# Holding Down's rows behind the product in the first feed-forward, and three of its tiles in the wide form

## The chip, the cores and the metric

The kernel runs on one core of a Trainium2 chip. The metric is the device time of one execution in microseconds (us), lower is better, as the median of several runs. PE is the tensor engine, DVE the vector engine, ACT the scalar engine, POOL the engine that issues some of the DMAs, SP the one that issues the others. PEld is the loading of weights into PE, which has its own rows in the trace.

## The reference

One decoder layer on 512 tokens of width 1024, in float32: a SwiGLU feed-forward, a mixer (dilated attention with 12 heads beside a gated linear recurrence), and a second SwiGLU feed-forward. Around each stand two RMS norms. The part that the change touches:

```python
def swiglu(x, w_gate, w_up, w_down):
    return (jax.nn.silu(x @ w_gate) * (x @ w_up)) @ w_down

f = swiglu(rms_norm(h, ffn1_norm_pre[l]), ffn1_w_gate[l], ffn1_w_up[l], ffn1_w_down[l])
h = h + 0.5 * rms_norm(f, ffn1_norm_post[l])
```

`w_gate` and `w_up` are 1024 x 2816, `w_down` is 2816 x 1024. 2816 is 22 tiles of 128 columns.

## The kernel before, in words

**Numbers in two parts.** Each float32 operand is split into a high part of a reduced format and a low part, the remainder (`split`, lines 302 to 304: one copy on ACT, one subtraction on DVE). A product is then three matmuls: high by high, high by low, low by high.

**Seven products for eight.** From tile 6 on in the first feed-forward, from tile 3 on in the second, the gate and up products of a tile of 128 columns are made together as a 2 x 2 block product with seven half-sized products p1 to p7 (a Strassen-Winograd scheme). Each of the seven runs over four slices of 128 of the contraction and has 256 columns of tokens. The weights are combined on DVE and split on ACT and DVE into seven forms (`w_forms`, lines 681 to 702), a tile ahead of their use. Partial sums of the seven are chained through PSUM banks: one bank is copied into another, and the next product adds onto the copy.

**Two forms of a tile's product.** The narrow form (`seven_on`, with `seventh`, lines 722 to 733) takes, for each of the seven products and each slice, three matmuls of 256 columns, at lines 730 to 732: 7 x 4 x 3 = 84 in a tile. It uses four PSUM banks of the tag `acc`, which has five. The wide form (`seven_wide`, from line 764) takes two matmuls for a slice, at lines 782 and 783: the high weights against the high and low tokens side by side (512 columns, into the two halves of a bank), and the low weights against the high tokens (256 columns, into the second half): 7 x 4 x 2 = 56 in a tile. It needs all five banks; its two halves are added up when a bank is read, by `fold` (ACT line 794, DVE line 796), `sum_of` (DVE lines 804 and 806) and `move` (ACT line 788, 512 columns). In the kernel before the wide form is in the mixer's query and key products and in tiles 9, 13 and 17 of the second feed-forward.

**Down in four steps.** The tiles are grouped in parts: 0 to 3, 4 to 7, 8 to 11, 12 to 15, and 16 to 21. The product of Down with the first four parts is also made with seven products, in four steps spread over the tiles behind the part (`STEPS_AT`). A step has two, two, one and two of the seven products; each is two groups of six matmuls of 512 columns (lines 1065 to 1067) into a bank of the tag `aux`, which has three. So the steps have 24, 24, 12 and 24 matmuls. A group's bank is first filled with the running sum by ACT ("seeding", line 1053), and copied out by ACT behind the group (line 1070). Behind the last part the sums are put together on DVE (`merge`, lines 1081 to 1087). In the first feed-forward the tiles and steps go: tile 9 and step 0, tile 10 and step 1, tile 11 and step 2, tile 12 and step 3, tile 13 and step 0, and so on.

**What sets the order.** The program is written with a scheduling layer: it orders the instructions of each engine by dependencies, by the order in the text and by priorities (`tc.high_priority`), and it inserts the waits on semaphores. `tc.issue_after(x)` keeps what stands under it behind the instruction `x`. `state["product"]` is the last matmul of the tile's product. In the second feed-forward (`n == 2`) Down's matmuls are held behind it; in the first they are free, and the scheduler may put them between those of the product. Weights come from DRAM over SP's queue in the order in which they are used, 512 KB at a time, through four buffers `raw`.

The tiles' outputs go through `into`, which forms the left operands of Down: on DVE at lines 925 to 935, and `split`.

Of the kernel before, what the change touches and what calls it, by code (L numbers as in the profile page):

```python
# [20 lines left out]
NF = 22  # L21
FF_PARTS = ((0, 4), (4, 8), (8, 12), (12, 16), (16, 22))
NSTD = {1: 6, 2: 3}
WIDE = {1: (), 2: (9, 13, 17)}

SEVEN = range(4)
STEPS_AT = {1: ((6, 7, 7, 8), range(9, 13), range(13, 17), range(17, 21)),
# [157 lines left out]
def hybrid_layer(ctx: ExitStack, tc: tile.TileContext, xT: bass.AP, xN: bass.AP, wst: bass.AP,  # L185
# [47 lines left out]
    state = {"g": 0, "i": 0, "off": 0, "raw": None, "ahead": AHEAD, "split": None}  # L233
# [78 lines left out]
    def tmp(name):  # L312
        return tpool.tile([P, T], F32, name=name, tag="t")
# [550 lines left out]
    def ffn(n, x, r, forms_x, apool, pss):  # L864
# [96 lines left out]
        def prod(f, w):  # L961
            g, u = tmp("g"), tmp("u")
            if f in WIDE[n]:
                seven_wide(t, w, *([x[:, h] for h in HALVES] for x in (g, u)), then=forms_left)
# [69 lines left out]
        def sum_at(p):  # L1034
            if p in outs:
                o, half, sign = outs[p]
                return quarter(o, half), sign
            return acts["ea"][:, extra.index(p)], 1.0

        def follows(a, p):  # L1040

            return a > 0

        def groups(i):
            return [(p, k) for p in SEVEN_STEPS[i] for k in range(2)]

        def seed(a, p, k):
            if "ea" not in acts:
                acts["ea"] = apool.tile([P, 4, 2, T], F32, name="ea", tag="e", bufs=1)
            ps = seeded[p, k] = aux_ps()  # L1050
            if follows(a, p):
                src, sign = sum_at(p)
                ACT.activation(ps, src[:, k], AF.Copy, scale=sign)

        def down7(a, i, w):
            x = sevens[a]
            gs = groups(i)
            for m, (p, k) in enumerate(gs):
                ps = seeded.pop((p, k))
                first = not follows(a, p)  # L1060
                for j in range(2):
                    xh, xl = (x[p][:, s_, j * HB + k * P:j * HB + k * P + P] for s_ in range(2))
                    wh, wl = (w[p][:, s_, j * T:(j + 1) * T] for s_ in range(2))
                    with tc.issue_after(state["product"]) if n == 2 else nullcontext():
                        PE.matmul(ps, xh, wh, start=first and j == 0, stop=False, skip_group_check=True)  # L1065
                        PE.matmul(ps, xh, wl, start=False, stop=False, skip_group_check=True)  # L1066
                        PE.matmul(ps, xl, wh, start=False, stop=j == 1, skip_group_check=True)  # L1067
                dst, sign = sum_at(p)
                with tc.high_priority(offset=EVAC):
                    ACT.activation(dst[:, k], ps, AF.Copy, scale=sign)  # L1070
                    if m + 3 < len(gs):
                        seed(a, *gs[m + 3])
            if a == SEVEN[-1]:
                merge(i)

        def merge(i):

            p1, p7, p6, p5 = (acts["ea"][:, k] for k in range(4))
            if i == 1:
                DVE.tensor_add(quarter(0, 0), quarter(0, 0), p1)  # L1080
                DVE.tensor_add(p6, p6, p1)
                DVE.tensor_add(p7, p7, p6)
                DVE.tensor_sub(quarter(0, 1), quarter(0, 1), p7)
                DVE.tensor_add(quarter(2, 0), quarter(2, 0), p6)
            if i == 2:
                DVE.tensor_add(quarter(2, 0), quarter(2, 0), p5)
                DVE.scalar_tensor_tensor(quarter(2, 1), p7, -1.0, p5, op0=ALU.mult, op1=ALU.subtract)
# [4 lines left out]
        for ev in ffn_order(n):  # L1092
            if ev[0] == "std":
                j = ev[1]
                while len(pss) < 2 * j + 2:
                    pss.append(acc_ps())
                    gemm(pss[-1], fetch(keys[len(pss) - 1]), x)
                with tc.high_priority(offset=EVAC if j == NSTD[n] - 1 else 0):
                    std_out(pss[2 * j], pss[2 * j + 1], j)

                for step in steps[j:] if j == min(NSTD[n], 4) - 1 else steps[j:j + 1]:
                    step()
            elif ev[0] == "prep":
                with ExitStack() as edges:
                    while behind:
                        edges.enter_context(tc.issue_after(behind.pop()))
                    forms[ev[1]] = w_forms(("gu", n, ev[1]))
            elif ev[0] == "prepd":
                forms[ev[1:]] = d_forms(*ev[1:])
                if n == 2:  # L1110
                    behind[:] = [state["split"], state["low"]]
            elif ev[0] == "seeds":
                for g in groups(ev[2])[:3]:
                    seed(ev[1], *g)
            elif ev[0] == "down7":
                down7(*ev[1:], forms.pop(ev[1:]))
            else:
                prod(ev[1], forms.pop(ev[1]))
# [773 lines left out]
```

## Time and profile before

| | us |
|---|---|
| median of 3 runs | 1206.48 (1205.55 to 1207.29) |
| the profiled execution | 1206.06 |
| its span, first to last instruction | 1204.3 |
| PE busy in the span | 1196.5 |
| DVE busy | 1039.5 |
| ACT busy | 838.7 |
| mean granted clock of PE | 0.998 |

A row of the timeline gives the start, the duration and the instruction. Matmuls are pipelined: the duration of a row reaches beyond the start of the next, so what a matmul costs in a dense stretch is the distance from its start to the next one's start. In the table by windows, a row has the window, its length, and for each engine the busy time with the number of instructions. Times in the texts count from the start of the span. The products of tiles 6 to 21 of the first feed-forward lie between 71.9 and 309.6 us, those of the second between 897.2 and 1165.2 us.

### The profile page before, as it was taken

The numbers are of one execution on the slowest core, as the hardware profiler recorded it, in microseconds if no ns is written. First come the engines' busy times: TensorE is split into PE (matmuls) and PEld (weight loads), VectorE is DVE, ScalarE is ACT, GpSimd is POOL, SyncE is SP. The second block draws the span as 40 slices with busy tenths as digits, with TensorE's granted clock in tenths as the row PEclk, the third lists the DMA queues.
The fourth block names the chain that finished last, engine by engine and source line by source line (L and its number), as shares of the span: only waits on it lengthen the run. The fifth ranks groups of instructions, "written<-read, shape, count | busy, mean of one in ns | idle before, by whom it ended". The sixth has DMA issues, their size and how long they took to land.

```text
span 1204.3 us, 18736 instructions
## 1 busy us (share of the span) xinstructions
PE 1196.5 (99%) x7138; PEld 1065.4 (88%) x7138; DVE 1039.5 (86%) x1641; ACT 838.7 (70%) x1455; POOL 26.1 (2%) x51
## 2 busy tenths in 40 slices
PE   9999999999999999999999999999999999999997
PEld 8899999999888889888888888888899989898996
DVE  7999888889689899999978899874798888889974
ACT  7566787887566676777836988734566687878763
POOL 0000000000011000000000000000100000000000
PEclk9999999999999999999999999999999999999999
DMA  7234343434725232322323432235443333333441
GB/s 268 88 95 132 126 140 108 139 111 153 248 102 165 71 97 88 97 82 86 107 73 119 170 115 100 80 113 189 144 141 106 123 123 123 123 125 122 140 176 70
DMA packets 45819, 149.77 MB, mean 124 GB/s; under 512 B 5152, under 2 KB 8608, under 8 KB 45728
## 3 DMA queue, kind: packets, MB, share of 16 engines
q1 hardware_dynamic: 38160, 131.09, 33.5%
q0 software_dynamic: 7280, 17.30, 4.3%
q8 instruction: 56, 0.92, 0.3%
q14 instruction: 35, 0.29, 0.1%
q10 hardware_dynamic: 288, 0.17, 0.0%
HBM read 138.06 MB, written 6.29 MB: 120 GB/s over the span
## 4 chain that ended last, share of the span: by engine, by line
PE 98%; DVE 1%; ACT 0%; issue 0%; DVEq 0%; ACTq 0%
PE acc L782 12%; PE acc L730 9%; PE acc L732 9%; PE acc L731 9%; PE acc L316 7%; PE acc L318 7%; PE acc L317 7%; PE acc L783 6%; PE aux L1066 4%; PE aux L1065 4%; PE aux L1067 4%; PE acc L432 2%; PE acc L433 2%; PE acc L434 2%; PE aux L433 1%; PE aux L432 1%
## 5 line engine op out<-in xcount | busy, mean ns | idle before, releaser
L304 DVE TENSOR_TENSOR w<-raw,w 128x1024 fp32r<-128x1024 f32 (+1 forms) x272 | 297.1, 1100 | 34.1 <-ACT w L303 32.6
L303 ACT ACTIVATE w<-raw 128x1024 fp32r<-128x1024 f32 (+1 forms) x272 | 259.0, 958 | 86.5 <-PE acc L318 46.4
L732 PE MATMUL acc<-big,w 128*128 128x256 f32 x788 | 223.3, 283 | 0.0
L731 PE MATMUL acc<-big,w 128*128 128x256 f32 x788 | 223.2, 283 | 0.0
L730 PE MATMUL acc<-big,w 128*128 128x256 f32 x788 | 223.2, 283 | 0.0
L782 PE MATMUL acc<-big,w 128*128 128x512 f32 x452 | 161.4, 397 | 0.1
L731 PEld LDWEIGHTS acc<-big,w 128*128 128x128 f32 x788 | 151.2, 192 | 1.3
L730 PEld LDWEIGHTS acc<-big,w 128*128 128x128 f32 x788 | 151.2, 192 | 1.2
L732 PEld LDWEIGHTS acc<-big,w 128*128 128x128 f32 x788 | 151.2, 192 | 0.0
L783 PE MATMUL acc<-big,w 128*128 128x256 f32 x452 | 127.4, 282 | 0.0
L782 PEld LDWEIGHTS acc<-big,w 128*128 128x128 f32 x452 | 85.0, 188 | 19.5 <-PE acc L783 0.4
L1065 PE MATMUL aux<-w,xf 128*128 128x512 f32 x224 | 87.6, 391 | 0.0
L1066 PE MATMUL aux<-w,xf 128*128 128x512 f32 x224 | 87.6, 391 | 0.0
L1067 PE MATMUL aux<-w,xf 128*128 128x512 f32 x224 | 87.2, 389 | 0.0
L783 PEld LDWEIGHTS acc<-big,w 128*128 128x128 f32 x452 | 85.4, 189 | 0.3
L304 DVE TENSOR_TENSOR w<-s,w 128x1024 fp32r<-128x1024 f32 x51 | 62.3, 1221 | 2.3 <-ACT w L303 2.0
L303 ACT ACTIVATE w<-s 128x1024 fp32r<-128x1024 f32 x51 | 53.8, 1056 | 8.1 <-PE acc L732 4.9
L316 PE MATMUL acc<-xf,w 128*128 128x512 f32 (+1 forms) x168 | 59.1, 353 | 0.0
L318 PE MATMUL acc<-xf,w 128*128 128x512 f32 (+1 forms) x168 | 58.5, 349 | 0.0
L317 PE MATMUL acc<-xf,w 128*128 128x512 f32 (+1 forms) x168 | 58.5, 349 | 0.0
L782 PE MATMUL acc<-rb,w 128*128 128x512 f32 x152 | 55.5, 397 | 0.0
L1067 PEld LDWEIGHTS aux<-w,xf 128*128 128x128 f32 x224 | 42.1, 188 | 8.9
(464 smaller groups left out, 2917.3 us busy)
## 6 DMA issues: line engine op xcount, KB each, us to landing
raw<-in_w SPq DMA_DIRECT2D x232, 512.0 KB, 3.5
big<-xf POOLq DMA_DIRECT2D x6, 512.0 KB, 3.3
gains<-in_rows POOLq DMA_DIRECT2D x5, 512.0 KB, 5.6
h<-in_x SPq DMA_DIRECT2D x8, 256.0 KB, 5.0
h<-in_xn POOLq DMA_DIRECT2D x4, 512.0 KB, 5.9
kept_m<-h POOLq DMA_DIRECT2D x4, 512.0 KB, 2.9
vals<-in_w SPq DMA_DIRECT2D x4, 512.0 KB, 6.2
h<-kept_m POOLq DMA_DIRECT2D x4, 512.0 KB, 5.9
```

The lines of the kernel that those rows point to most:

```text
L303: state["split"] = ACT.activation(dh, src, AF.Copy).ins
L304: state["low"] = DVE.tensor_sub(dl, src, dh.bitcast(F32)).ins
L316: PE.matmul(ps, wh, xh, start=first, stop=False)
L317: PE.matmul(ps, wh, xl, start=False, stop=False)
L318: PE.matmul(ps, wl, xh, start=False, stop=last)
L730: PE.matmul(ps, wh, xh, start=start and k == 0, stop=False, skip_group_check=True)
L731: PE.matmul(ps, wh, xl, start=False, stop=False, skip_group_check=True)
L732: state["product"] = PE.matmul(ps, wl, xh, start=False, stop=k == 3, skip_group_check=True).ins
L782: PE.matmul(part, wh, at(BOTH, k), start=start and k == 0, stop=False, skip_group_check=True)
L783: last = PE.matmul(cross, wl, at(0, k), start=False, stop=k == 3, skip_group_check=True)
L1065: PE.matmul(ps, xh, wh, start=first and j == 0, stop=False, skip_group_check=True)
L1067: PE.matmul(ps, xl, wh, start=False, stop=j == 1, skip_group_check=True)
```

## The change

Two edits. The first puts tiles 10, 14 and 18 of the first feed-forward into the wide form. The second holds Down's matmuls behind the last matmul of the tile's product in both feed-forwards.

```diff
@@ -21,7 +21,7 @@
 NF = 22
 FF_PARTS = ((0, 4), (4, 8), (8, 12), (12, 16), (16, 22))
 NSTD = {1: 6, 2: 3}
-WIDE = {1: (), 2: (9, 13, 17)}
+WIDE = {1: (10, 14, 18), 2: (9, 13, 17)}
 
 SEVEN = range(4)
 STEPS_AT = {1: ((6, 7, 7, 8), range(9, 13), range(13, 17), range(17, 21)),
@@ -1061,7 +1061,7 @@
                 for j in range(2):
                     xh, xl = (x[p][:, s_, j * HB + k * P:j * HB + k * P + P] for s_ in range(2))
                     wh, wl = (w[p][:, s_, j * T:(j + 1) * T] for s_ in range(2))
-                    with tc.issue_after(state["product"]) if n == 2 else nullcontext():
+                    with tc.issue_after(state["product"]):
                         PE.matmul(ps, xh, wh, start=first and j == 0, stop=False, skip_group_check=True)
                         PE.matmul(ps, xh, wl, start=False, stop=False, skip_group_check=True)
                         PE.matmul(ps, xl, wh, start=False, stop=j == 1, skip_group_check=True)
```

The wide form is chosen in `prod`, where the list is read:

```python
if f in WIDE[n]:
    seven_wide(t, w, *([x[:, h] for h in HALVES] for x in (g, u)), then=forms_left)
```

In the built program PE has 84 matmuls fewer. Its order is otherwise the same but for one matmul: in the kernel before, the first matmul of Down's step 0 behind tile 6 stands after 12 of that tile's 84 matmuls; now all 24 stand behind the tile. Behind the first feed-forward no engine's order differs.

## The prediction

> **What bounds the kernel now.** I read the page first, its busy times and the chain that ended last; then PE's timeline, for the true cost of a matmul; then the table by windows for the two forms with the Down step behind them; last, DVE's and ACT's timelines, since these must follow a faster PE.
>
> From the page:
>
> ```profile
> span 1204.3 us, 18736 instructions
> PE 1196.5 (99%) x7138; PEld 1065.4 (88%) x7138; DVE 1039.5 (86%) x1641; ACT 838.7 (70%) x1455; POOL 26.1 (2%) x51
> ...
> PE 98%; DVE 1%; ACT 0%; issue 0%; DVEq 0%; ACTq 0%
> ...
> L730 PE MATMUL acc<-big,w 128*128 128x256 f32 x788 | 223.2, 283 | 0.0
> L782 PE MATMUL acc<-big,w 128*128 128x512 f32 x452 | 161.4, 397 | 0.1
> ```
>
> PE is busy in 99% of the span and is 98% of the chain: what PE issues is what the kernel takes. The trap stands in the last two lines (lines 731 and 732 have the same mean as 730). By these durations a slice costs 3 x 283 = 849 ns in the narrow form and 397 + 283 = 680 ns in the wide one; 28 slices in 3 tiles would save 14 us. But the rows overlap, so the price must be read from starts. PE's timeline, at tile 10 (narrow) and at tile 9 of the second feed-forward (wide):
>
> ```profile
> 136.78 0.28 PE L730 MATMUL acc<-big,w 128*128 128x256 f32 x1
> 136.89 0.28 PE L731 MATMUL acc<-big,w 128*128 128x256 f32 x1
> ...
> 146.85 0.40 PE L1065 MATMUL aux<-w,xf 128*128 128x512 f32 x1
> ```
>
> ```profile
> 982.29 0.39 PE L782 MATMUL acc<-big,w 128*128 128x512 f32 x1
> ...
> 992.17 0.40 PE L1065 MATMUL aux<-w,xf 128*128 128x512 f32 x1
> ```
>
> The first two rows start 0.11 us apart and last 0.28 each. The narrow tile's 84 matmuls take 146.85 - 136.78 = 10.07 us (120 ns each), the wide tile's 56 take 992.17 - 982.29 = 9.88 us (353 ns a slice). Both stream 768 columns a slice; only a small cost for each matmul goes.
>
> **The change, part by part.** *The wide form on PE.* By windows: tile 10, the 24 matmuls of Down behind it, and the wide tile. Behind the length stand the busy times of PE, PEld, DVE, ACT and POOL with their counts, then the granted clock and the DMA's share and rate:
>
> ```profile
> 136.78:146.85 10.07, 10.07 (x85) 10.07 (x84) 8.25 (x11) 6.62 (x13) 0.00 (x0) 1.00 0.40 123
> 146.85:152.32 5.47, 5.47 (x26) 4.52 (x25) 4.61 (x7) 5.44 (x10) 0.00 (x0) 1.00 0.34 121
> 982.29:992.17 9.88, 9.88 (x58) 8.57 (x56) 8.23 (x16) 7.33 (x14) 0.00 (x0) 1.00 0.46 159
> ```
>
> A tile saves 10.07 - 9.88 = 0.19 us, three save **0.57 us**, all of it on PE's path, as PE has no gap in these windows. The granted clock is 1.00 in all.
>
> The Trainium skill's page "TensorE: Matmul & The Clock Gate", section "Wait — 56ns, not 53.3ns?", puts a fixed cost of about 2.5 ns on each warm matmul beside its columns; by that rule 84 matmuls fewer would save an estimated 0.2 us instead. The rows, with 6.8 ns for each matmul saved (0.57 us over 84), decide here.
>
> *The hold.* It has one matmul to move:
>
> ```profile
> 73.33 0.40 PE L1065 MATMUL aux<-w,xf 128*128 128x512 f32 x1
> ...
> 82.20 0.40 PE L1066 MATMUL aux<-w,xf 128*128 128x512 f32 x1
> ```
>
> Everywhere else in the first feed-forward Down already stands behind the product. The 0.23 us of this matmul move to 82 us and cost the same there. In the built order it now waits for PE's own semaphore: if that is the matmul just before it, PE pays at most the row of that one, 0.28 us, once; at the least nothing. I take 0.1 us. Its group ends as before, so ACT's copy behind it is not later. Queued behind it are 23 matmuls of the same step, which tile 7 follows. SP keeps its loads in the stream's order (only the `raw` buffers that some take are swapped) and POOL's queue doesn't change, so no DMA is moved past another.
>
> *What the wide form adds on DVE and ACT.* Narrow has on DVE four instructions of 256 columns (lines 970, 975 and twice 980); wide has eight of 256 (796, 804, 806) and one of 512 (989). The steps between starts on DVE:
>
> ```profile
> 145.27 1.22 DVE L304 TENSOR_TENSOR w<-raw,w 128x1024 fp32r<-128x1024 f32 x1
> 146.40 0.42 DVE L970 TENSOR_TENSOR g<-acc,c 128x256 f32<-128x256 f32 x1
> 146.73 0.68 DVE L697 TENSOR_TENSOR raw<-s,raw 128x512 f32<-128x512 f32 x1
> 147.33 0.42 DVE L980 SCALAR_TENSOR_TENSOR tt<-g,acc 128x256 f32<-128x256 f32 x1
> ```
>
> That is 0.33 us for 256 columns, 0.60 for 512, 1.13 for 1024. The wide form adds 4 x 0.33 + 0.60 = **1.92 us of DVE** a tile. On ACT six copies of 256 become three moves and a silu of 512 and four folds of 256. Their steps stand here, in the wide tile of the second feed-forward:
>
> ```profile
> 986.78 0.58 ACT L788 ACTIVATE acc<-acc 128x512 f32<-128x512 f32 x1 [0.68 <-PE acc L783]
> 987.27 0.38 ACT L794 ACTIVATE c<-acc 128x256 f32<-128x256 f32 x1
> 987.53 1.06 ACT L303 ACTIVATE w<-sum 128x1024 fp32r<-128x1024 f32 x1
> ...
> 989.69 0.61 ACT L788 ACTIVATE acc<-acc 128x512 f32<-128x512 f32 x1
> ```
>
> 0.49 for a move, 0.26 for a fold: 4 x 0.49 + 4 x 0.26 - 6 x 0.26 = 1.4 us more. Who waits for them? First p7 and p4 inside the tile, which add onto the moved banks. p4 starts 24 slices into the tile, 982.29 + 24 x 0.353 = 990.76; its move ends at 990.30: 0.46 us to spare. In the changed order of tile 10 ACT has the same instructions ahead of that move, so I cost it at nothing. Second, the forms of the next tile: at tile 10 DVE now makes the low part of tile 11's first form only after the last fold. The tile ends at 136.78 + 9.88 = 146.66; a fold on ACT and one on DVE take about 1 us, the form 1.2, so it is done by 148.9. PE needs it behind Down, at 146.66 + 5.47 = 152.1. Down's step is the cover. Third, the tight place, behind tile 18:
>
> ```profile
> 255.66:271.20 15.54, 15.54 (x109) 14.59 (x108) 12.47 (x18) 12.02 (x23) 0.00 (x0) 1.00 0.40 119
> 271.20:284.02 12.82, 12.82 (x97) 12.33 (x96) 12.55 (x15) 9.36 (x17) 0.00 (x0) 1.00 0.30 103
> 284.02:299.56 15.54, 15.54 (x109) 14.58 (x108) 14.89 (x21) 11.88 (x21) 1.19 (x2) 1.00 0.62 190
> 1129.24:1144.77 15.53, 15.53 (x110) 14.57 (x109) 15.53 (x19) 11.48 (x21) 0.54 (x1) 1.00 0.40 132
> ```
>
> DVE has 3.07, 0.27 and 0.65 us free in the stretches of tiles 18, 19 and 20, where `merge` comes on top. What PE needs from it there is line 1086, which ACT turns into the seed of a group of Down:
>
> ```profile
> 257.85 1.22 DVE L304 TENSOR_TENSOR w<-raw,w 128x1024 fp32r<-128x1024 f32 x1
> ...
> 289.07 1.22 DVE L1086 TENSOR_TENSOR facc<-facc,ea 128x1024 f32<-128x1024 f32 x1
> ...
> 291.23 0.59 ACT L1053 ACTIVATE aux<-facc 128x512 f32<-128x512 f32 x1
> ...
> 296.84 0.39 PE L1065 MATMUL aux<-w,xf 128*128 128x512 f32 x1
> ```
>
> In the changed order 47 DVE instructions stand from the first of these to line 1086: 19 of 1024, 14 of 512, 14 of 256 columns, 19 x 1.13 + 14 x 0.60 + 14 x 0.33 = 34.5 us, so it ends at 292.4 without waits. With the 1 to 3 us of waiting that a wide tile's folds bring, it ends near 294 to 295.3; with 0.6 us for the seed, 295 to 296.1. PE needs it 0.2 us sooner than before, the tile being shorter, at 296.6. Margin 0.5 to 1.6 us: nothing to pay if I am right, one microsecond if my waits are short by as much. I take 0.1 us.
>
> The sum: -0.57 + 0.1 + 0.1 = -0.4 us. The profiled execution took 1206.06 us (span 1204.3 and 1.8 around it), 0.42 below the median 1206.48. From the median: **1206.1 us**. Nothing under 0.2% (2.4 us) can be told from no change, so this is "the same".
>
> **The rivals.** *DVE falls behind: slower.* The place is Down's step behind tile 20, and the first forms behind each wide tile. If none of the added 1.92 us is absorbed in three tiles, PE pays 5.8 us: 1206.5 - 0.6 + 5.8 = **1211.7 us**. It decides once more than 3 us, half of it, come through to PE. For it: 0.27 and 0.65 us free behind tile 18, and the `raw` buffers, released later, delay loads on which DVE waits in turn. Against it: in the last row of that fence DVE has no free time at all in 15.53 us, behind the wide tile 17 of the second feed-forward, and PE has no gap there.
>
> *The moves come late.* A 1.06 us conversion ahead of a move, begun just before it, would overrun the 0.46 us to spare by 0.6 us. Once in each of the three tiles is 1.8 us: **1207.9**, still within 0.2%. None of the three wide tiles of the second feed-forward shows it, in their 9.88 us.
>
> *The weight loads set the pace: faster.* In the narrow window PEld is busy for 10.07 of 10.07 us, in the wide one for 8.57 of 9.88. If loads bound, 56 for 84 would bring a tile from 10.07 to 6.7 us: 3.4 us less, 10 us in three: **1196**. The wide tile's 9.88 us speak against it. The Trainium skill's page "Trainium Kernel Development and Optimization", section "Performance Expectations", calls matmul busy time a bad metric because matmuls are pipelined, and the busy share of weight loads a good one; the first half agrees with the overlapping rows here, the second would point to this rival.
>
> *The change doesn't do what it says.* For the hold this holds nearly: it moves one matmul. The time is then that of the forecast.
>
> **How the numbers follow.** Forecast, PE's small gain with at most 1 us given back: 0.80. Late moves: 0.05, also "same". DVE behind: 0.12, of which 0.10 end beyond 2.4 us. Weight loads, or a gain that I don't see: 0.03. So faster 0.03, same 0.87, slower 0.10. The range runs from 1205.0 (the whole 0.57 us, and the 0.9 us by which a median of three may lie low, as the runs spread from 1205.55 to 1207.29) to 1208.3 (the late moves and a part of DVE's 5.8 us); about 0.15 lies outside.
>
> **What would show it.** Right: PE's starts 9.88 us apart from first product to first Down matmul at the three tiles, no row of PE between 137 and 310 us starting late, 24 Down matmuls together from 82 us, ACT's move 0.4 us before p4. Wrong: gaps in front of line 1065 near 296 us or of lines 730 and 782 behind the wide tiles, with DVE named as the releaser; a wide tile much shorter than 9.88 us; or a stage behind the first feed-forward with another length, where no engine's order has changed.

## The result, and the profile after

| | before | changed |
|---|---|---|
| median of 14 runs, us | 1206.41 (1205.55 to 1207.29) | 1209.24 (1207.93 to 1209.83) |
| ratio, 95% interval | | 1.0022 (1.0015 to 1.0029) |
| span of the profiled execution, us | 1204.3 | 1207.1 |
| first product matmul of tile 6 to the same of tile 21, us | 227.67 | 230.64 |

The change costs 2.8 us, 0.22%; the forecast was a gain of 0.4. The last row of the table is called "the stretch" below: it holds everything that the change touches, 299.56 - 71.89 before and 302.25 - 71.61 after, and it grew by 2.97 us. Behind it nothing moves much.

From the page of the changed kernel, the lines that answer to those of before:

```profile
span 1207.1 us, 18604 instructions
...
PE 1197.3 (99%) x7054; PEld 1060.0 (88%) x7054; DVE 1044.7 (87%) x1656; ACT 842.2 (70%) x1461; POOL 26.1 (2%) x51
...
PE 89%; DVE 6%; DMA 2%; ACT 1%; issue 1%; DVEq 0%; ACTq 0%
...
L730 PE MATMUL acc<-big,w 128*128 128x256 f32 x716 | 203.0, 283 | 1.7 <-ACT c L744 1.7
```

PE was 98% of the chain and is 89%: DVE, ACT and the loads have come onto it. And line 730, which had no idle time, has 1.7 us, released by line 744, a copy on ACT. The table by windows of the changed kernel: the wide tile 10 and its Down step, tile 12, tile 16, and Down behind tile 20 (columns as before: length, busy times with counts, granted clock, DMA):

```profile
136.49:146.37 9.88, 9.88 (x58) 8.57 (x56) 7.65 (x11) 7.42 (x13) 0.00 (x0) 1.00 0.41 122
146.37:151.83 5.46, 5.46 (x26) 4.51 (x25) 5.46 (x11) 5.17 (x9) 0.00 (x0) 1.00 0.18 69
164.65:176.28 11.63, 10.59 (x86) 10.18 (x84) 10.86 (x15) 7.97 (x15) 0.00 (x0) 1.00 0.40 137
...
225.45:236.60 11.15, 10.46 (x85) 10.17 (x84) 10.62 (x15) 7.87 (x14) 0.00 (x0) 1.00 0.42 143
296.08:302.25 6.17, 5.76 (x27) 4.44 (x26) 6.17 (x9) 5.88 (x10) 0.00 (x0) 1.00 0.69 241
```

The wide tile takes the forecast 9.88 us and its Down step 5.46. Tile 12, which is narrow and two tiles further on, takes 11.63 us instead of 10.07; tile 16 takes 11.15; Down behind tile 20 takes 6.17 instead of 5.47. So 1.56 + 1.08 + 0.70, with 0.23 inside tile 20, are lost, and 3 x 0.19 won: +3.0 us, which is the growth of the stretch. PE's timeline in tile 12 has the place:

```profile
170.55 0.28 PE L732 MATMUL acc<-big,w 128*128 128x256 f32 x1
171.86 0.39 PE L730 MATMUL acc<-big,w 128*128 128x256 f32 x1 [1.03 <-ACT c L744]
```

It is the first matmul of the fifth product, p7, which adds onto a bank that ACT must have copied before (`c6 = copy(b)` in `seven_on`). It comes 1.19 us too late, and the step behind it takes 0.10 us more than usual. The other 0.27 us of tile 12 are lost at the first matmuls of p6, which adds onto a bank that ACT copies too (`copy(b, y)`). In tile 16 the split is 0.94 at p7 and 0.14 at p6. The chain of waits of the changed kernel around p7's first matmul in tile 12:

```profile
164.22 1.15 DVE w L304
165.37 0.02 issue
165.38 3.74 DMA raw<-in_w
169.12 0.02 issue
169.15 0.69 DVE s L693
169.84 0.61 DVE tt L935
170.45 0.02 issue
170.48 0.03 ACT xf L303
170.50 0.94 issue
171.44 0.38 ACT c L744
171.81 0.04 issue
171.86 0.39 PE acc L730
```

In these rows ACT keeps to the order of its queue. Line 303 there (`xf<-tt`, 1024 columns, a left operand of a Down step to come) waits for line 935 on DVE. The copy is behind it, although its own input, p6, had been complete on PE for a while. ACT's timeline in this place, in the kernel before and in the changed one:

```profile
168.31 1.06 ACT L303 ACTIVATE xf<-tt 128x1024 fp32r<-128x1024 f32 x1 [0.28 <-DVE tt L935]
169.27 0.77 ACT L744 ACTIVATE c<-acc 128x256 f32<-128x256 f32 x2
```

```profile
168.09 0.37 ACT L744 ACTIVATE c<-acc 128x256 f32<-128x256 f32 x1
170.48 1.06 ACT L303 ACTIVATE xf<-tt 128x1024 fp32r<-128x1024 f32 x1 [2.01 <-DVE tt L935]
171.44 0.37 ACT L744 ACTIVATE c<-acc 128x256 f32<-128x256 f32 x1
```

Before, the copies ended at 170.04 us, and p7 was due at 165.14 + 48 x 0.12 = 170.90: the queue had 0.86 us of slack. Now ACT stands idle for 2.01 us in front of the conversion and PE for more than one behind it. Why line 935 is late shows on DVE, before and after:

```profile
163.58 0.42 DVE L980 SCALAR_TENSOR_TENSOR tt<-g,u 128x256 f32<-128x256 f32 x1
164.04 0.69 DVE L928 TENSOR_TENSOR tt<-tt 128x512 f32<-128x512 f32 x1
...
167.59 0.69 DVE L935 SCALAR_TENSOR_TENSOR tt<-tt 128x512 f32<-128x512 f32 x1
168.19 1.22 DVE L304 TENSOR_TENSOR w<-raw,w 128x1024 fp32r<-128x1024 f32 x1
```

```profile
163.80 0.42 DVE L980 SCALAR_TENSOR_TENSOR tt<-g,u 128x256 f32<-128x256 f32 x1
164.13 1.82 DVE L304 TENSOR_TENSOR w<-raw,w 128x1024 fp32r<-128x1024 f32 x2
165.87 0.68 DVE L928 TENSOR_TENSOR tt<-tt 128x512 f32<-128x512 f32 x1
...
169.15 0.69 DVE L693 TENSOR_TENSOR s<-s,raw 128x512 f32<-128x512 f32 x1 [0.25 <-DMA raw<-in_w]
169.76 0.68 DVE L935 SCALAR_TENSOR_TENSOR tt<-tt 128x512 f32<-128x512 f32 x1
```

Line 980 is 0.22 us late. Behind it the built order now has two conversions of weights, 1.73 us, in front of line 928; before, the one of 512 columns came ahead of line 980, and one of 1024 columns behind line 935. So line 935 ends 2.16 us later by the clock, 2.65 later counted from the tile's first matmul. Of that, 1.13 us (one conversion of 1024 columns more) is order; the other 1.5 us are a DVE that runs behind and its waits for loads. The chain above shows one such load, which starts only when DVE has done line 304 at 165.37 us.

The copy that p6 needs in tile 12 is late by order as well: ACT's work runs without a break from the silu of tile 11 (line 971 at 162.38 us, which had waited 2.79 us for line 970 on DVE) to this copy at 167.27, and now holds a conversion of 512 columns that before came ahead of the silu.

### The profile page after: what moved, and what is told of

The parts are those of the page before. It is cut to its first block, busy times and chain, and to the rows that moved or that the text cites. A ratio compares the mean times of both kernels' runs of the same rounds, so it can differ in the third digit from the quotient of the medians.

```text
span 1207.1 us, 18604 instructions
## 1 busy us (share of the span) xinstructions
PE 1197.3 (99%) x7054; PEld 1060.0 (88%) x7054; DVE 1044.7 (87%) x1656; ACT 842.2 (70%) x1461; POOL 26.1 (2%) x51
## 4 chain that ended last, share of the span: by engine, by line
PE 89%; DVE 6%; DMA 2%; ACT 1%; issue 1%; DVEq 0%; ACTq 0%
PE acc L782 12%; PE acc L316 7%; PE acc L318 7%; PE acc L317 7%; PE acc L730 7%; PE acc L732 7%; PE acc L731 7%; PE acc L783 6%; PE aux L1065 3%; PE aux L1066 3%; PE aux L1067 3%; DVE w L304 2%; DMA raw<-in_w 2%; PE acc L434 2%; PE acc L432 2%; PE acc L433 2%
## 5 line engine op out<-in xcount | busy, mean ns | idle before, releaser
L730 PE MATMUL acc<-big,w 128*128 128x256 f32 x716 | 203.0, 283 | 1.7 <-ACT c L744 1.7
L731 PE MATMUL acc<-big,w 128*128 128x256 f32 x716 | 202.6, 283 | 0.0
L732 PE MATMUL acc<-big,w 128*128 128x256 f32 x716 | 202.6, 283 | 0.0
L782 PE MATMUL acc<-big,w 128*128 128x512 f32 x524 | 186.8, 397 | 0.0
L783 PE MATMUL acc<-big,w 128*128 128x256 f32 x524 | 147.2, 281 | 0.0
L730 PEld LDWEIGHTS acc<-big,w 128*128 128x128 f32 x716 | 137.2, 192 | 3.6 <-ACT c L744 2.1
L731 PEld LDWEIGHTS acc<-big,w 128*128 128x128 f32 x716 | 137.2, 192 | 1.1
L732 PEld LDWEIGHTS acc<-big,w 128*128 128x128 f32 x716 | 137.2, 192 | 0.0
L782 PEld LDWEIGHTS acc<-big,w 128*128 128x128 f32 x524 | 98.4, 188 | 22.9 <-issue 0.3
L783 PEld LDWEIGHTS acc<-big,w 128*128 128x128 f32 x524 | 98.8, 189 | 0.4
L788 ACT ACTIVATE acc<-acc 128x512 f32<-128x512 f32 x75 | 44.2, 590 | 11.6 <-PE acc L783 10.0
```

The source lines that it names most:

```text
L730: PE.matmul(ps, wh, xh, start=start and k == 0, stop=False, skip_group_check=True)
L731: PE.matmul(ps, wh, xl, start=False, stop=False, skip_group_check=True)
L732: state["product"] = PE.matmul(ps, wl, xh, start=False, stop=k == 3, skip_group_check=True).ins
L782: PE.matmul(part, wh, at(BOTH, k), start=start and k == 0, stop=False, skip_group_check=True)
L783: last = PE.matmul(cross, wl, at(0, k), start=False, stop=k == 3, skip_group_check=True)
```

## The experiments

They are told in the order of the argument. Each ratio is to runs of the kernel before that were taken together with it. The stretch is read from the profiled execution of each, and "p7's gap" is the distance on PE in front of the first matmul of p7, beyond the usual 0.12 us. In the second feed-forward the profiled executions differ by up to 1.3 us even where the order is that of before (its tiles 3 to 21 take 267.80 us in before and 269.08 in early_subs), through gaps of up to 0.9 us at changing places (last section). So a span says less than the stretch.

| run | ratio (95% interval) | stretch, us | against before |
|---|---|---|---|
| before | | 227.67 | |
| changed kernel | 1.0022 (1.0015 to 1.0029) | 230.64 | +2.97 |
| after_again | 1.0024 (1.0014 to 1.0035) | 229.85 | +2.18 |
| hold_only | 1.0001 (0.9993 to 1.0010) | 227.66 | -0.01 |
| wide_only | 1.0008 (0.9999 to 1.0017) | 228.96 | +1.29 |
| tile10 | 1.0009 (1.0000 to 1.0018) | 228.20 | +0.53 |
| more_dve | 1.0003 (0.9994 to 1.0012) | 228.38 | +0.71 |
| delay_forms | 1.0012 (1.0003 to 1.0021) | 229.54 | +1.87 |
| late_forms | 1.0004 (0.9995 to 1.0013) | 228.96 | +1.29 |
| merge_only | 1.0016 (1.0007 to 1.0025) | 228.45 | +0.78 |
| late_merge | 1.0010 (1.0001 to 1.0019) | 228.57 | +0.90 |
| late_merge1 | 0.9998 (0.9989 to 1.0007) | 227.67 | 0.00 |
| early_subs | 1.0013 (1.0004 to 1.0022) | 229.51 | +1.84 |
| pool_sums | 1.0075 (1.0062 to 1.0088) | 237.55 | +9.88 |

### Which part of the change costs

**hold_only**: the changed kernel without the wide tiles.

```diff
-WIDE = {1: (10, 14, 18), 2: (9, 13, 17)}
+WIDE = {1: (), 2: (9, 13, 17)}
```

> The hold alone: the first feed-forward keeps the narrow form in all of its tiles, and Down's rows are held behind the last product. Theory (the microseconds lost come from the wide form's work on DVE, which ACT's queue passes on to PE; the hold is free): the time of the kernel before within 0.3 us, span 1204.3 plus or minus 0.3, the tile at 71.6 us again 10.07 us to its first Down matmul and 5.46 us of Down behind it, no stall of PE in tiles 12 and 16. Rival (the hold itself costs, since PE then waits for its own last product and Down's 23 rows no longer fill gaps): about +2 to +3 us, with the stalls of the changed kernel in tiles 12 and 16 in place.

1206.61 us against 1206.63, and the stretch is that of before. Windows of tile 6 and the Down step behind it in this run, with the one matmul moved:

```profile
71.64:81.71 10.07, 10.07 (x85) 10.07 (x84) 9.89 (x13) 7.38 (x11) 0.00 (x0) 1.00 0.14 54
81.71:87.18 5.47, 5.47 (x26) 4.51 (x25) 5.47 (x9) 4.72 (x8) 0.00 (x0) 1.00 0.08 13
```

The hold alone is free. The span, 1205.0, missed the expected 1204.3 plus or minus 0.3 by a gap of 0.8 us in the second feed-forward, where the order is that of before.

**after_again**: the changed kernel unaltered.

> The changed kernel once more, unaltered. In the run with line 1086 taken earlier, whose DVE and ACT orders are the changed kernel's up to tile 20, the stalls of tiles 12 and 16 were 0.79 and 0.56 us and not 1.55 and 1.07. Theory (the size of these stalls varies between executions, since DVE there waits for loads): stalls at the same two places, between 0.5 and 1.6 us each, 0.5 to 1 us around tile 20, span 1205.8 to 1207.2, ratio 1.001 to 1.003. Rival (line 1086's priority itself made them smaller): 1.5 and 1.1 us within 0.2.

1209.29 us. p7's gaps are 1.19 us in tile 12 and 0.85 in tile 16, and Down behind tile 20 takes 6.01 us. The places are the same, and the sizes vary by some tenths from one execution to the next.

**wide_only**: the changed kernel without the hold.

```diff
-                    with tc.issue_after(state["product"]):
+                    with tc.issue_after(state["product"]) if n == 2 else nullcontext():
```

> The wide form in tiles 10, 14 and 18 without the hold: two of Down's 24 matmuls may then stand behind the first product in tiles 6, 12 and 16. Theory (the wide form pays, the hold is free): slower than the kernel before as the changed kernel is, ratio 1.001 to 1.0025, span 1206.0 to 1207.3, with stalls of 0.5 to 1.5 us in tiles 12 and 16. Rival (the hold takes from PE the rows that could fill these gaps): the kernel before within 0.5 us, span 1204.0 to 1204.8.

1207.64 us; both theories had half of it. Line 935 is as late as in the changed kernel (5.63 us into tile 12), but in tiles 12 and 16 two matmuls of Down now stand in front of p5, and PE's timeline has the gap there:

```profile
165.98 0.28 PE L732 MATMUL acc<-big,w 128*128 128x256 f32 x1
166.93 0.73 PE L1065 MATMUL aux<-w,xf 128*128 128x512 f32 x2 [0.67 <-ACT w L303]
```

PE waits 0.83 us for these two, whose weights are also converted on ACT; their own 0.46 us fall into time that would be lost anyway, and p7 then comes without a gap. In all 0.94 us are lost in tile 12, 0.47 in tile 16 and 0.49 in Down behind tile 20. So, as these rows read, the hold, which is free by itself, takes 0.46 us of useful filling from each of the two tiles once the wide form has opened a gap there. The medians say the same (1.65 us between this run and after_again), with intervals that overlap.

**tile10**: one wide tile.

```diff
-WIDE = {1: (10, 14, 18), 2: (9, 13, 17)}
+WIDE = {1: (10,), 2: (9, 13, 17)}
```

> The changed kernel with one wide tile, 10. DVE's and ACT's orders are the changed kernel's up to tile 13 and the narrow kernel's from there. Theory (each wide tile delays PE two tiles on, and the delay is then worked off): a stall of 0.5 to 1.5 us in tile 12 and none above 0.2 us in tiles 16 and 20, span 1204.5 to 1205.6. Rival (the lateness adds up from tile to tile): stalls in tile 16 or behind tile 20 too.

Windows of tile 12 and of tile 16 in this run:

```profile
165.42:176.24 10.82, 10.33 (x86) 10.12 (x85) 10.30 (x15) 7.63 (x14) 0.00 (x0) 1.00 0.42 147
225.60:235.67 10.07, 10.07 (x85) 10.06 (x84) 10.00 (x14) 8.04 (x15) 0.00 (x0) 1.00 0.39 133
```

Tile 12 loses 0.75 us, nothing else is late, and the stretch grows by 0.75 - 0.19. The lateness does not add up: it is worked off within four tiles. The span, 1206.0, is over the expected range through the second feed-forward again.

### What passes the lateness on

**more_dve**: hold_only with scratch work on DVE in tiles 10, 14 and 18, in no use for the output.

```diff
                         DVE.tensor_add(u[:, hi], b, c5)
+                        if n == 1 and f in (10, 14, 18):
+                            more = tmp("more")
+                            for _ in range(4):
+                                DVE.tensor_add(more[:, lo], u[:, hi], c5)
+                            DVE.tensor_add(more[:, hi], u[:, hi], c5)
+                            DVE.tensor_add(more, more, more)
```

> The narrow form in all tiles of the first feed-forward, with the hold, and in tiles 10, 14 and 18 five additions of 256 columns and one of 512 on DVE that compute nothing of use (scratch): 5 x 0.33 + 0.60 = 2.25 us of DVE a tile, somewhat more than the wide form's 1.92. Theory (DVE's added time is the cause, and its delay reaches PE through ACT's queue two tiles on): stalls of PE in tiles 12 and 16 of 0.5 to 1.6 us each and near tile 20, span 1206.0 to 1208, ratio 1.001 to 1.003, without any wide tile. Rival (the wide form itself is the cause: its moves between banks on ACT, or banks held longer): no stall in tiles 12 and 16, ratio 1.000 plus or minus 0.001.

1206.79 us, 1.0003: the theory falls in the form in which it stood there, and the rival's ratio holds. Its reason, the wide form itself, is not what the next two runs show. 2.25 us more on DVE at each of the three tiles cost 0.71 us in all (0.35 in tile 12, the rest in tiles 16 and 20). In tile 12 it is lost at p6: the copy that p6 needs stands behind work on ACT without a break, which began when a wait of 1.17 us for line 970 on DVE was over. So a part of DVE's delay does reach PE through ACT's queue. Line 935 ends 3.83 us into tile 12 instead of 3.14. That is 0.69 later, under the 0.86 of slack, and p7 has no gap. Between 155 and 205 us DVE's order is that of before here: no conversion moves in front of line 928, and waits of DVE take up most of the 2.25 us (before, it stood idle for 2.5 us between 147 and 160). DVE's time alone is not what the change costs.

**delay_forms**: hold_only, the narrow form in all tiles of the first feed-forward, with scratch additions between lines 934 and 935, and the two copies kept behind the conversion in ACT's queue.

```diff
                     DVE.scalar_tensor_tensor(q[:, 0], q[:, 3], -1.0, q[:, 0], op0=ALU.mult, op1=ALU.subtract)
+                    if n == 1 and a in (2, 3):
+                        more = tmp("more")
+                        with tc.high_priority(offset=EVAC):
+                            for _ in range(a - 1):
+                                DVE.tensor_add(more, q[:, 0], q[:, 1])
                     DVE.scalar_tensor_tensor(q[:, 1], q[:, 0], -1.0, q[:, 2], op0=ALU.mult, op1=ALU.subtract)
...
                         form(two, tt[:, 0:2].rearrange("p q j t -> p (q j t)"))
+                        if n == 1 and a in (2, 3):
+                            state["behind"] = state["split"]
...
-            with tc.high_priority(offset=EVAC):
+            with tc.high_priority(offset=EVAC), tc.issue_after(behind) if behind else nullcontext():
                 state["copied"] = ACT.activation(dst, ps, AF.Copy).ins
...
+        behind = None
         seventh(t, w, "p1", b, True)
         copy(b, y)
+        behind = state.pop("behind", None)
         seventh(t, w, "p5", z, True)
...
+        behind = None
         then()
```

> Narrow form everywhere (the hold alone), and between lines 934 and 935 scratch additions of 512 columns on DVE, one ahead of tile 12 and two ahead of tile 16, with a conversion of weights of 1.13 us that the order then puts there too; ACT keeps its order in this place: the conversion that waits for line 935 stands ahead of the two copies, of which PE's p7 needs the second. Counted from the order, line 935 comes 0.60 + 1.13 - 0.60 = 1.13 us later in tile 12 and 2 x 0.60 + 1.13 = 2.33 us later in tile 16. In the kernel before, the second copy ends at 170.04 us and p7 is due at 165.14 + 48 x 0.12 = 170.90: 0.86 us of slack. Theory (a late line 935 reaches PE through that queue, less the slack): stalls at p7 of 0.3 us in tile 12 and 1.5 us in tile 16, and none of lines 782 or 1065. Rival (PE's stalls in the changed kernel have another cause, and such a delay is absorbed): no stall above 0.2 us in either tile.

Line 935 comes 1.18 us later in tile 12 and 2.46 in tile 16, counted from the tile's start, and the tiles lose 0.34 and 1.18 us, at p7's first two matmuls. ACT and PE in tile 12 of this run, in whose kernel line 935 is line 943:

```profile
169.78 1.06 ACT L303 ACTIVATE xf<-tt 128x1024 fp32r<-128x1024 f32 x1 [1.42 <-DVE tt L943]
170.74 0.64 ACT L744 ACTIVATE c<-acc 128x256 f32<-128x256 f32 x2
```

```profile
171.06 0.28 PE L732 MATMUL acc<-big,w 128*128 128x256 f32 x1
171.43 0.39 PE L730 MATMUL acc<-big,w 128*128 128x256 f32 x1
```

Without a single wide tile, a late line 935 makes a stall of the changed kernel's kind, beyond a slack of about 0.9 us and of the size that was expected (0.3). This is the link, shown by itself. Tile 16 doesn't show it as cleanly:

```profile
229.73 1.06 ACT L303 ACTIVATE w<-sum 128x1024 fp32r<-128x1024 f32 x1 [1.67 <-PE acc L732]
230.70 1.04 ACT L303 ACTIVATE xf<-tt 128x1024 fp32r<-128x1024 f32 x1
231.64 0.64 ACT L744 ACTIVATE c<-acc 128x256 f32<-128x256 f32 x2
```

Here the built order puts a conversion of weights ahead of the one that waits for line 935, against what was expected of ACT's order, and ACT stands idle for 1.67 us in front of it until PE is done with p6. Line 935 ends at 230.60, so the second conversion would have started at nearly the same time if the first one had not been there. But it would also have started then if line 935 had been early. The 1.18 us can't be put down to one of the two. It is the same kind of queue all the same: conversions that wait stand ahead of the copies. PE starts p7 at 232.06, when the first of the two copies is done (232.01).

The other 0.34 us of the stretch's 1.87 are lost in Down behind tile 7 and in tile 8, ahead of the additions; why, the run doesn't show.

Narrow tiles 12 and 16 of other runs lie on one line with tile 12, as long as a gap at p6 has not already put p7 off (in more_dve it had, by 0.35 us):

| run, tile | line 935 ends after the tile's start, us | the copy for p7 ends | p7's gap |
|---|---|---|---|
| before, 12 | 3.14 | 4.90 | 0 |
| more_dve, 12 | 3.83 | 5.47 | 0 |
| delay_forms, 12 | 4.32 | 5.95 | 0.25 |
| merge_only, 16 | 4.80 | 6.16 | 0.47 |
| tile10, 12 | 4.99 | 6.36 | 0.65 |
| merge_only, 12 | 5.04 | 6.41 | 0.71 |
| after_again, 16 | 5.20 | 6.56 | 0.85 |
| after_again, 12 | 5.52 | 6.87 | 1.19 |

p7 is due 48 x 0.12 = 5.76 us into the tile, and the gap is the copy's end plus 0.05 to 0.08 less 5.76 in each row that has one.

**late_forms**: the changed kernel, with the conversions queued behind the last copy, as the second feed-forward has them.

```diff
-                    with tc.high_priority(offset=AHEAD), tc.issue_after(state["copied"]) if n == 2 else nullcontext():
+                    with tc.high_priority(offset=AHEAD), tc.issue_after(state["copied"]) if n == 2 or a else nullcontext():
...
-                if n in (2,):
+                if n == 2 or a:
                     later.append(rest)
```

> The changed kernel, with one thing moved: in the first feed-forward, as in the second, the conversions that follow a Down group (line 303 on ACT, 1024 columns, which waits for line 935 on DVE) are queued behind the last copy of the product and not between its last two. Theory (a late DVE stops ACT at that conversion, with the copy that PE's p7 needs behind it): the stalls of tiles 12 and 16, 1.55 and 1.07 us, go; the 0.95 us around tile 20 stays, since the merge's seed is not touched; span about 1204.5 against 1207.1, so within 0.3 us of the kernel before. Rival (DVE is simply too full by some 3 us, and the wait only shows where PE meets it first): the stalls reappear a little later, at the first forms of tiles 13 and 17 or in Down, and the span stays at 1206.5 or more. Second rival (the conversion comes too late for those who need it, Up's tiles behind): new stalls of lines 782 or 730 with line 303 as the releaser.

1206.69 us, no longer to be told from before. Line 935 ends 4.93 us into tile 12 (with 4.99, tile10 lost 0.65 us at p7) and 6.32 into tile 16, and neither tile has a gap at p7. The window of tile 12:

```profile
164.95:175.02 10.07, 10.07 (x85) 10.07 (x84) 9.72 (x15) 7.21 (x13) 0.00 (x0) 1.00 0.45 158
```

Tile 12 is back at 10.07 us: the cut link takes the stall away, though DVE is still late. But a new gap of 0.86 us comes up at p6 of tile 16 (and 0.28 us are lost in tile 17), in this run's timeline of PE:

```profile
227.93 0.39 PE L730 MATMUL acc<-tx,w 128*128 128x256 f32 x1 [0.70 <-ACT acc L744]
```

There the copy of p1 stands in ACT's queue behind five microseconds of conversions and Down's copies without a break, which began only when a wait of 3.48 us for line 970 on DVE was over: the same mechanism, one copy earlier. The first rival is right in part, then: some of the lateness shows at another place. With Down behind tile 20 (6.10 us) this makes the stretch 1.29 us longer than before, where the theory had about 0.4.

### The seed behind tile 20, and both mends

**merge_only**: the changed kernel, with line 1086 taken earlier.

```diff
-                DVE.tensor_add(quarter(2, 0), quarter(2, 0), p5)
+                with tc.high_priority(offset=AHEAD):
+                    DVE.tensor_add(quarter(2, 0), quarter(2, 0), p5)
```

> The changed kernel, with line 1086 (DVE's addition onto which the seed of a Down group behind tile 20 is built) given the priority that the forms have, so that DVE takes it earlier. Theory (two places pay, and this mends the smaller one): the 0.73 us in front of Down's line 1065 near 299 us go, with some of the 0.22 us in tile 20; tiles 12 and 16 keep their 1.55 and 1.07 us; span about 1206.1 to 1206.4. Rival (DVE is short of time in total, so what is taken forward makes something else late): the span stays at 1207.1, with the forms of tile 20 or 21 now late for PE.

Down behind tile 20 is back at 5.47 us and tile 20 at 10.07, so the place and its price hold. In tiles 12 and 16, where DVE's and ACT's orders are the changed kernel's, only 0.79 and 0.56 us are lost, and the stretch grows by 0.78; 1207.92 us, 1.3 less than the changed kernel, with intervals of the ratios that overlap.

**late_merge** has both mends.

```diff
-                    with tc.high_priority(offset=AHEAD), tc.issue_after(state["copied"]) if n == 2 else nullcontext():
+                    with tc.high_priority(offset=AHEAD), tc.issue_after(state["copied"]) if n == 2 or a else nullcontext():
...
-                if n in (2,):
+                if n == 2 or a:
...
-                DVE.tensor_add(quarter(2, 0), quarter(2, 0), p5)
+                with tc.high_priority(offset=AHEAD):
+                    DVE.tensor_add(quarter(2, 0), quarter(2, 0), p5)
```

> The changed kernel with both mends at once: the conversions behind a Down group queued behind the last copy, and line 1086 taken earlier on DVE. Theory (all that the change costs goes through these two places, and the 1.92 us of DVE a tile can be absorbed): PE keeps the 3 x 0.19 us of the wide form, span about 1203.7, 0.6 us below the kernel before, ratio about 0.9995. Rival (DVE short of time in total): the stalls move elsewhere, span 1205.5 or more.

1207.70 us: a miss. The stretch is +0.90, not -0.5: 0.29 us are lost in tile 12, 0.52 in 16, 0.13 in 17 and 0.53 in 20, at matmuls that add onto a bank which ACT copies. The products of the second feed-forward take 1.7 us longer than before. Line 1086 is in both feed-forwards, and the priority reorders DVE in the second as well; but since executions with the order of before differ there by up to 1.3 us, the run doesn't show that this is the cause.

**late_merge1**: both, with line 1086's priority in the first feed-forward alone. The edit is shown against late_merge.

```diff
-                with tc.high_priority(offset=AHEAD):
+                with tc.high_priority(offset=AHEAD) if n == 1 else nullcontext():
```

> Both mends in the first feed-forward alone: in the run with both, the priority of line 1086 held in the second feed-forward too, where DVE's order changed in 22 rows and PE stalled 0.54 us near 1140 us. Theory (that stall and a part of the span come from there): the first feed-forward ends 0.6 us behind the kernel before, or earlier, as in that run; the second is as in the kernel before; span 1204.3 to 1205.2. Rival (the second feed-forward's stalls are scatter between executions, whatever its order): stalls of 0.3 to 0.9 us there in this run too, span up to 1206.

1206.36 us, 0.9998. The stretch is 227.67: 0.57 us won by three wide tiles, about as much lost in tiles 15 and 16 (0.28 and 0.32). It is 2.9 us faster than the changed kernel, with intervals that don't overlap, and the same as the one before. The rival is right too: with before's order the second feed-forward had gaps of 0.31 and 0.37 us in this run.

### What did not help

**early_subs**: the changed kernel, with lines 928, 934 and 935 at the priority of the copies.

```diff
-                    DVE.tensor_sub(q[:, 1], q[:, 3], q[:, 1])
+                    with tc.high_priority(offset=EVAC) if n == 1 else nullcontext():
+                        DVE.tensor_sub(q[:, 1], q[:, 3], q[:, 1])
...
-                    DVE.scalar_tensor_tensor(q[:, 0], q[:, 3], -1.0, q[:, 0], op0=ALU.mult, op1=ALU.subtract)
-                    DVE.scalar_tensor_tensor(q[:, 1], q[:, 0], -1.0, q[:, 2], op0=ALU.mult, op1=ALU.subtract)
+                    with tc.high_priority(offset=EVAC) if n == 1 else nullcontext():
+                        DVE.scalar_tensor_tensor(q[:, 0], q[:, 3], -1.0, q[:, 0], op0=ALU.mult, op1=ALU.subtract)
+                        DVE.scalar_tensor_tensor(q[:, 1], q[:, 0], -1.0, q[:, 2], op0=ALU.mult, op1=ALU.subtract)
```

> The changed kernel, with lines 928, 934 and 935 on DVE given the copies' priority in the first feed-forward: in tiles 12 and 16 line 935 then stands ahead of line 693 (0.60 us and its wait for a load), and the conversion of 512 columns comes earlier on both engines. Theory (what counts is how late line 935 is): the p7 stalls of tiles 12 and 16 fall by 0.6 to 0.9 us against the changed kernel's of the same call, and those at p6 (0.28 us) go; the place behind tile 20 keeps its 0.5 to 1 us; span 0.8 to 1.8 us shorter. Rival (the load that line 693 waits for, or the folds in the wide tile, set the stall and not the order of line 935): stalls as in the changed kernel.

In tile 12 line 935 ends 4.50 us into the tile instead of 5.52 in after_again, p7's gap falls from 1.19 to 0.06 us, and the tile loses 0.26 instead of 1.28. So the lateness of line 935 sets this gap. Tile 16 loses 1.05 all the same, 0.81 of it now at p6, behind a copy on ACT. Line 935 comes no earlier there (5.29 us into the tile, 5.20 in after_again), and p7's gap is down to 0.05 only because p6 has put p7 off. Tile 20 and Down behind it lose 1.09, where after_again lost 0.54. The span was to be 0.8 to 1.8 us shorter and is 1207.1 against 1206.5: a miss. The median is 1208.28 us, 1.0 less than after_again's, with intervals that overlap.

**pool_sums**: the changed kernel, with lines 1007 and 1012 on POOL.

```diff
-                    DVE.tensor_add(sd, g0, u0)
+                    (nc.gpsimd if n == 1 and a in (1, 2, 3) else DVE).tensor_add(sd, g0, u0)
...
-                    DVE.tensor_add(sd, sd, u1)
+                    (nc.gpsimd if n == 1 and a in (1, 2, 3) else DVE).tensor_add(sd, sd, u1)
```

> The changed kernel, with two additions of 1024 columns (lines 1007 and 1012, the running sum of Down's weights) in each of the parts at tiles 9, 13 and 17 taken from DVE to POOL: 2 x 1.13 = 2.26 us of DVE less a part, which is about what a wide tile adds. Theory (DVE's time is the cause): the stalls in tiles 12 and 16 and near tile 20 go, or fall below 0.3 us each, span 1203.7 to 1204.7. Rival (late loads into the raw buffers, not DVE's time, are the cause): the stalls stay at 0.8 us or more in tiles 12 and 16. Second rival (an addition of POOL is so long, or slows DVE so much, that the forms made from the sum come late): a new stall at Down's line 1065 or 1066, and a span over 1207.

1215.05 us: the second rival, and more; p7's gaps in tiles 12 and 16 stay as well (1.08 and 0.95 us). POOL's addition and DVE beside it:

```profile
129.35 3.31 POOL L1012 TENSOR_TENSOR sum<-sum,raw 128x1024 f32<-128x1024 f32 x1 [13.01 <-DVE w L304]
```

```profile
130.33 0.42 DVE L975 TENSOR_TENSOR u<-acc,c 128x256 f32<-128x256 f32 x1
130.66 2.56 DVE L697 TENSOR_TENSOR raw<-s,raw 128x512 f32<-128x512 f32 x1
```

The addition takes 3.31 us for DVE's usual step of 1.13, and line 697 takes 2.56 us for its usual 0.68 while it runs. DVE is busy for 1049.6 us in all, more than with the additions its own (1044.7). The run can't say what a relieved DVE would bring.

## Why the prediction was wrong

**Right.** PE gains the forecast 0.19 us a tile by the wide form: all three wide tiles take 9.88 us. So the durations of the rows were rightly set aside, and so was the rival of the weight loads: 56 loads for 84 brought no more than that. The hold moves one matmul and costs nothing by itself (forecast 0.1). The moves in the wide tiles come in time, and so do the first forms of tiles 11, 15 and 19.

**Wrong: "Who waits for them?"** This step lists three that wait for the slower DVE and ACT: the products in the wide tile, the next tile's forms, and the seed behind tile 20. It leaves out the left operands of Down (lines 928 to 935 and their conversion), for which PE has ample time and ACT's queue has not. What is queued behind the waiting conversion, the copy for p7, has 0.86 us of slack. In the changed kernel this path costs 2.2 us, at p7 in tiles 12 and 16. The other 0.4 us lost in these two tiles are at p6, whose copy is late in the same queue; the step left that out too. The forecast had nothing for either.

**Wrong in part: the cost of DVE as a sum of instructions.** I took 1.92 us a tile and looked for the places that would feel it. The size is about right (DVE's busy time grew by 5.2 us, 1.7 a tile), but more_dve shows that a like amount, put in so that no conversion moves in front of line 928, costs 0.7 us in three tiles. The wide form also changed the built order of DVE two tiles on: a conversion of weights now stands ahead of line 928. My step looked at the order in and right behind the wide tiles, and behind tile 18, but not there.

**Mis-sized: the tight place.** Line 1086 was to come after 34.5 us of work and 1 to 3 of waits; it ended 37.81 us after the start of the first of the 47 instructions, so there were 3.3 of waits. The seed was to take 0.6 us more; from the end of line 1086 at 297.88 to PE's start at 299.39 it took 1.5, as ACT had other work queued. 0.3 + 0.9 against a margin of 0.5 leaves 0.7, and the Down step lost 0.70. The sum also has a slip, which doesn't bear on this: 292.4 plus 1 to 3 us is 293.4 to 295.4, not 294 to 295.3, and the margin ran from 0.6 to 2.6 us.

**The rival.** *DVE falls behind* had the sign, the engine and the size from which it decides (about 3 us), at 0.12. Of its places one held (behind tile 20). The argument against it, that DVE has no free time behind tile 17 of the second feed-forward and PE no gap, was read past the reason: there the conversions stand behind the copies. late_forms puts them so in the first, and the medians no longer differ measurably from before, though its stretch is still 1.29 us longer.

**Open.** How line 935's lateness beyond the 1.13 us of order divides into DVE's own time and late loads isn't settled. A fifth `raw` buffer, which might tell, wasn't tried.

## What to carry to other kernels

In an engine's in-order queue, what counts is not whether the waiting instruction is urgent but what stands behind it: look, for each instruction that a slower engine will delay, at the next one in the waiting queue and at its slack. Added work on an engine is not only so many microseconds: compare the built order some tiles on, as far as the lateness lives. A hold that is free in a dense stream can take away the filler as soon as something opens a gap, as the rows of wide_only read.

## What was not expected of the hardware

**An addition on POOL stops some instructions of DVE.** While line 1012 ran on POOL, line 697 (both inputs in the on-chip memory) took 2.56 us for 0.68, and it ended 0.56 us behind POOL's; line 975, one of whose inputs is an `acc` bank, kept its 0.42. In all six places with such an addition line 697 ends 0.55 to 0.56 us behind it. The Trainium skill's page "SBUF — State Buffer", section "Who interferes with whom", says that a DVE instruction with two SBUF inputs contends with a GpSimd instruction that reads SBUF, and that the ports which the two share are locked by one of them at a time; these rows agree, as line 697 ends about one usual step (0.60 us) behind the addition.

**Equal orders, unequal gaps.** hold_only has before's order on DVE and ACT, and on PE but for one matmul of tile 6. In its second feed-forward PE lost 0.78 us at one place where before lost nothing. ACT's timeline there, before and in hold_only (whose clock runs 0.2 us ahead):

```profile
1122.09 1.06 ACT L303 ACTIVATE w<-raw 128x1024 fp32r<-128x1024 f32 x1 [0.77 <-DMA raw<-in_w]
```

```profile
1123.01 1.06 ACT L303 ACTIVATE w<-raw 128x1024 fp32r<-128x1024 f32 x1 [1.91 <-DMA raw<-in_w]
...
1125.19 0.37 ACT L744 ACTIVATE acc<-acc 128x256 f32<-128x256 f32 x1
```

A load came 1.1 us later, and the copy for PE stood behind the waiting conversion and one more in ACT's queue. The load was started at the same point (1117.54 us before, 1117.33 in hold_only), but took 5.66 us to land and not 4.52. Why the same load lands so differently, the runs don't show.
